# Gate and up of a hybrid decoder block: a phase's third pair of weight tiles is issued behind the reads of the last phase's banks

## The chip, the core and the metric

The kernel runs on one core of one Trainium2 chip. The metric is the device time of one execution in microseconds (us); the time before is the median of three runs. The engines are TensorE (PE, with its weight loads as PEld), VectorE (DVE), ScalarE (ACT), GpSimd (POOL) and SyncE (SP). Each works through its own queue of instructions in the order in which they were written out, and the queues meet through semaphores.

## The reference

The reference is one layer of a decoder block in float32, with 512 tokens and a model width of 2048: a mixer of two head groups, a cross attention over 256 memory tokens, and a SwiGLU. What the change touches is the first half of the SwiGLU:

```
hf = rms_norm(x, g_ffn)
gg, uu = jnp.split(hf @ w_gu, 2, axis=-1)        # w_gu: 2048 x 11264
return x + (jax.nn.silu(gg) * uu) @ w_down        # w_down: 5632 x 2048
```

## The kernel before

The products of a large matrix are taken with seven block products in place of eight (a scheme of Strassen's kind), so weights are first added and subtracted among each other, and the results are put together from several banks. Each product is made in three matmuls to keep float32 accuracy: every operand is split into a high and a low part in the matmul's type (`split`, L128 on ACT for the cast to the high part, L129 on DVE for the low part), and `mm3` (L171 to L173) adds high x high, high x low and low x high. In a row of the profile a tile `qh` is thus a high part and `ql` a low part; `qh` has five buffers and `ql` four.

Gate and up is the loop `for n in range(NB)` (L1204), eleven turns of 512 columns of gate and 512 of up. A turn has two phases, each a call of `phase` (L1135). A phase goes over eight pairs of rows of the weights, `kp` = 0 to 7. The document calls what belongs to one `kp` a pair: pair 0, 1, 2 and so on, so that the third pair is pair 2 (`kp == 2`).

In the first phase `weights_1` (L1108) loads 768 KB for a pair into a tile `raw` (three buffers), subtracts in place (L1111), makes a split of 1024 columns (a), adds (L1113), keeps a copy of the sum (L1115), and makes a second split of 1024 columns (b). A pair then has four products of six matmuls, 24 in all, into the banks "s", "mm", "t" and "mm"/"o". In the second phase `weights_2` (L1119) loads 512 KB, subtracts the kept sum (L1122), and makes one split of 1024 columns and one of 512; a pair has three products, 18 matmuls, which are added onto three of the same sets of banks.

In a phase the pairs 0 and 1 are multiplied together, product by product; then each later pair follows by itself. At the end of the first phase ACT copies a bank (L1214) and DVE adds up the others (L1215, L1217, L1219, two instructions each). At the end of the second phase ACT applies the SiLU to one set of banks (L1229) and DVE adds the others onto sums kept in SBUF (L1231, L1233, two instructions each); L1235 to L1239 finish the values of gate times up. The second phase of a turn also turns the results of the turn before (`turn`, L1166 to L1181), stores them, and starts sums of quarters of `w_down` on POOL's queue (L1195, L1200).

The order of the instructions on each engine is not written by hand. A planner makes it when the program is built: it takes an instruction whose inputs and buffers it expects to be ready, by priority. Priority is the place in the program, moved forward by an offset: a pair's loads and splits are 150 places ahead (`AHEAD`), the reads of the banks at the end of a phase 170 (`EVICT`). Each engine then works in that order, whatever is in fact ready.

Of the kernel before, what the change touches and what calls it, by code (L numbers as in the profile page):

```python
# [13 lines left out]
AF = mybir.ActivationFunctionType  # L14
# [12 lines left out]
AHEAD = 150  # L27
# [28 lines left out]
def hybrid_block(ctx: ExitStack, tc: tile.TileContext, x_t, mem_t, sv, cmat, umask, w_a, w_r67, w_v, w_vg, w_v3,  # L56
                 w_vsw, w_gk2, w_c1, w_c2, w_out, w_cq, w_ck, w_cv, w_co, w_gu, w_down, y_t):
    nc = tc.nc
    V, S, G, PE = nc.vector, nc.scalar, nc.gpsimd, nc.tensor
# [14 lines left out]
    def small(tag, bufs):  # L74
        return sb([128, 32], tag, bufs)
# [7 lines left out]
    def bank(tag):  # L83
        return psp.tile([128, 512], F32, name=tag, tag=tag, bufs={"mm": 3, "s": 2, "t": 2, "o": 1}[tag])
# [54 lines left out]
    class Weights:  # L139
# [9 lines left out]
        def load(self):  # L149
            a = len(self.parts) * self.cut  # L150
            n = min(self.cut, self.cols - a)
            if self.raws:
                raw = sb([128, 1280], *self.raws[len(self.parts)])
            else:
                raw = sb([128, 1024], "w", 2)
            hi, lo = sb([128, 1024], "wh", 3, F32R), sb([128, 1024], "wl", 3, F32R)
            for b in range(0, n, self.step):
                c = slice(b, min(b + self.step, n))
                nc.sync.dma_start(raw[:, c], self.src[:, a + c.start:a + c.stop])
                split(hi[:, c], lo[:, c], raw[:, c])  # L160
            self.parts.append((hi, lo))
# [13 lines left out]
    def part(pair, a, n):  # L175
        return pair[0][:, a:a + n], pair[1][:, a:a + n]
# [50 lines left out]
    def token_norm_col(ss, n, tiles):  # L227
        ps = bank("s")
        for i in range(tiles):
            mm(ps[:, i:i + 1], ss[:, 128 * i:128 * i + 128], one, start=True, stop=True)  # L230
        rc = const.tile([128, 8], F32, name="rc", tag="rc", bufs=4)[:, :tiles]
        inv_rms(rc, ps[:, :tiles], n, const.tile([128, 32], F32, name="rt", tag="rt", bufs=1)[:, :tiles])
        return rc
# [192 lines left out]
    rc2 = small("rc2", 1)[:, :NT]  # L426
# [581 lines left out]
    def sb1(tag, dt=F32):  # L1008
        return pool1.tile([128, COLS2.get(tag, 512)], dt, name=tag, tag=tag, bufs=BUFS2[tag])
# [5 lines left out]
    def split_cols(raw, a, n):  # L1015
        hi, lo = sb1("qh", F32R), sb1("ql", F32R)
        split(hi[:, :n], lo[:, :n], raw[:, a:a + n])
        return hi, lo
# [31 lines left out]
    def sb2(tag, dt=F32):  # L1050
        return pool2.tile([128, COLS2.get(tag, 512)], dt, name=tag, tag=tag, bufs=BUFS2[tag])
# [56 lines left out]
    def weights_1(n, kp):  # L1108
        raw = sb1("raw")
        nc.sync.dma_start(raw[:, :1536], w_gu[n, kp, :, 512:2048])  # L1110
        V.tensor_sub(raw[:, 0:1024], raw[:, 0:1024], raw[:, 512:1536])  # L1111
        a = split_cols(raw, 0, 1024)
        V.tensor_add(raw[:, 1536:2048], raw[:, 0:512], raw[:, 1024:1536])  # L1113
        kept[kp] = sb1("T2")
        S.copy(kept[kp], raw[:, 1536:2048])  # L1115
        b = split_cols(raw, 1024, 1024)
        return part(b, 512, 512), part(b, 0, 512), part(a, 0, 512), part(a, 512, 512)

    def weights_2(n, kp):  # L1119
        raw = sb1("raw")  # L1120
        nc.sync.dma_start(raw[:, :1024], w_gu[n, kp, :, 0:1024])
        V.tensor_sub(raw[:, 1024:1536], raw[:, 0:512], kept[kp])  # L1122
        a = split_cols(raw, 0, 1024)
        b = split_cols(raw, 1024, 512)
        return part(a, 0, 512), part(b, 0, 512), part(a, 512, 512)

    def product(banks, kp, a, w, start, stop, again):
        for i in range(2):
            mm3(banks[i], part(combos[kp], 256 * a + 128 * i, 128), w, start=start, stop=stop, again=again)
# [2 lines left out]
    PHASE_1 = (4, 0, 5, 3)  # L1132
    PHASE_2 = (1, 2, 6)

    def phase(load, banks, plan, middle, last, fresh, ahead, extra):  # L1135

        ws = {}

        def weights(kp):
            with tc.high_priority(offset=AHEAD if kp > 1 else ahead):  # L1140
                ws[kp] = load(kp)

        for kp in range(2):
            weights(kp)
        for p, a in enumerate(plan):
            for kp in range(2):
                product(banks[p], kp, a, ws[kp][p], fresh and kp == 0, False, not fresh)
        for kp in range(2, KP):
            weights(kp)
            for p in last if kp == KP - 1 else middle:  # L1150
                product(banks[p], kp, plan[p], ws[kp][p], False, kp == KP - 1, not fresh)
            for go in extra.get(kp, ()):
                go()
# [6 lines left out]
    def turn(hs, n, k, tag="s"):  # L1160
        def go():
            ps = [bank(tag), bank(tag)]
            for f in range(2):
                c = 256 * k + 128 * f
                for i in range(NT):
                    PE.transpose(ps[f][:, 128 * i:128 * i + 128], hs[i][:, c:c + 128], ident)  # L1166

            e, o, a, b = [sb1("T2") for _ in range(4)]
            S.copy(e, ps[0])
            S.copy(o, ps[1])  # L1170
            x, y = slice(0, 256), slice(256, 512)
            h = V.tensor_sub(a[:, x], e[:, y], o[:, y])
            V.tensor_sub(b[:, x], e[:, x], e[:, y])
            V.tensor_sub(a[:, y], a[:, x], e[:, x])
            V.tensor_add(b[:, y], o[:, x], a[:, y])
            d = hd[n // 3].rearrange("q (p c) -> q p c", p=7)
            c = 512 * (n % 3) + 256 * k
            S.dma_start(d[:, 0, c:c + 256], e[:, x])
            for p, t in ((1, o), (3, a), (5, b)):
                S.dma_start(d[:, p:p + 2, c:c + 256], t.rearrange("q (p c) -> q p c", p=2))  # L1180
            if n < NB - 1:  # L1181
                add_quarters(2 * n + k, h)
        return go
# [17 lines left out]

    rc2 = []
    hs = None
    for n in range(NB):  # L1204
        b1 = [bank("mm"), bank("mm")]
        bu = [bank("s"), bank("s")]
        b2 = [bank("t"), bank("t")]
        b3 = [bank("mm"), bank("o")]
        phase(lambda kp: weights_1(n, kp), (bu, b1, b2, b3), PHASE_1, (2, 3, 1, 0), (1, 0, 2, 3), True,
              AHEAD if n else 40, {})  # L1210
        u, c22 = [sb2("C") for _ in range(2)], [sb2("C") for _ in range(2)]
        with tc.high_priority(offset=EVICT):
            for i in range(2):
                S.copy(u[i], b1[i])  # L1214
                V.tensor_add(u[i], u[i], bu[i])  # L1215
            for i in range(2):
                V.tensor_add(c22[i], u[i], b2[i])  # L1217
            for i in range(2):
                V.tensor_add(c22[i], c22[i], b3[i])  # L1219
        if n == 0:  # L1220
            rc2 = token_norm_col(ss, D, NT)
        extra = {}
        if hs:
            extra = {2: [turn(hs, n - 1, 0)], 4: [turn(hs, n - 1, 1)]}
        phase(lambda kp: weights_2(n, kp), (b1, b2, b3), PHASE_2, (1, 0, 2), (0, 1, 2), False, AHEAD, extra)
        g1, g2 = [sb2("C") for _ in range(2)], [sb2("C") for _ in range(2)]
        with tc.high_priority(offset=EVICT):
            for i in range(2):
                S.activation(g1[i], b1[i], AF.Silu, scale=rc2[:, i:i + 1])  # L1229
            for i in range(2):  # L1230
                V.tensor_add(g2[i], u[i], b2[i])  # L1231
            for i in range(2):
                V.tensor_add(u[i], u[i], b3[i])  # L1233
        for i in range(2):
            S.activation(g2[i], g2[i], AF.Silu, scale=rc2[:, 2 + i:3 + i])  # L1235
        for i in range(2):
            V.scalar_tensor_tensor(g1[i], u[i], rc2[:, i:i + 1], g1[i], op0=OP.mult, op1=OP.mult)
        for i in range(2):
            V.scalar_tensor_tensor(g2[i], c22[i], rc2[:, 2 + i:3 + i], g2[i], op0=OP.mult, op1=OP.mult)  # L1239
        hs = g1 + g2  # L1240
# [91 lines left out]
    banks = [None, [bank(t) for t in SETS[1]]]  # L1332
# [3 lines left out]
    for step, plan in enumerate(STEPS):  # L1336
# [3 lines left out]
        elif step == 1:  # L1340
            banks = [[bank(t) for t in SETS[r]] for r in rs_]
        elif step == 2:
            banks[1] = [bank(t) for t in SETS[1]]
        else:
            banks = [[bank(t) for t in SETS[r]] for r in rs_]
# [30 lines left out]
        elif step == 2:  # L1376
            u = [sb2("C") for x in range(4)]
# [123 lines left out]
```

## Time and profile before

| | us |
|---|---|
| median of 3 runs (lowest, highest) | 2417.41 (2416.54, 2420.03) |
| the profiled execution | 2416.0 |
| its span, first to last instruction | 2413.9 |
| PE busy | 2325.7 (96%) |
| DVE busy | 1672.6 (69%) |
| ACT busy | 1183.2 (49%) |
| mean granted clock of TensorE | 0.987 of full speed |

Busy time is counted from an instruction's start to its end, with waits left out. Matmuls overlap, so that a busy TensorE is not one at its peak: in the dense stretches of this stage a matmul starts every 0.227 us, though each row gives 0.39 us. A number in brackets behind a row of a timeline is the time for which the engine stood idle before it, and what it waited for. The eleven turns of gate and up lie between about 1048 and 1965 us of the span.

### The profile page before, as it was taken

To read this page: it belongs to the slowest core of one execution; us is meant where nothing else is said; L and a number is where in the kernel's file an instruction comes from. 1 tells how busy PE (TensorE), PEld (TensorE's weight loads), DVE (VectorE), ACT (ScalarE), POOL (GpSimd) and SP (SyncE) were. 2 spreads that over 40 slices of the span, in tenths; PEclk is the share of its full clock that TensorE was granted. 3 is DMA by queue.
4 is the path that set the end of the run, shared out by engine and by line. 5 is a ranking of instruction groups with operands and counts; after the bars stand their busy time and mean duration, and the time that the engine had idled before them with its cause. 6 is when DMAs were issued, how large, how long until landed. Compare 5 with 4: busy or idle time off the path is not lost.

```text
span 2413.9 us, 29614 instructions
## 1 busy us (share of the span) xinstructions
PE 2325.7 (96%) x10954; PEld 1923.0 (80%) x10954; DVE 1672.6 (69%) x2522; ACT 1183.2 (49%) x1787; POOL 130.3 (5%) x187
## 2 busy tenths in 40 slices
PE   8999999999999999979999999999999998999999
PEld 7798888888887887768877787777778777888887
DVE  6647876667786335698777777778877875775685
ACT  6633454556675225565444444444544456444542
POOL 0000000000000000110001000100100000000000
PEclk9999999999999999989999999999999999999999
DMA  6432233423225332564557666765766689676763
GB/s 232 150 107 70 84 114 122 146 81 101 92 92 175 122 130 85 165 197 144 175 174 222 201 187 202 224 185 175 234 201 191 201 306 331 229 255 227 256 252 144
DMA packets 131681, 421.33 MB, mean 175 GB/s; under 512 B 13488, under 2 KB 33968, under 8 KB 127312
## 3 DMA queue, kind: packets, MB, share of 16 engines
q1 hardware_dynamic: 82048, 325.05, 38.8%
q0 software_dynamic: 26064, 70.00, 12.2%
q10 hardware_dynamic: 23424, 24.39, 2.9%
q8 instruction: 86, 1.41, 0.2%
q14 instruction: 59, 0.48, 0.1%
HBM read 376.92 MB, written 84.67 MB: 191 GB/s over the span
## 4 chain that ended last, share of the span: by engine, by line
PE 79%; DMA 9%; DVE 6%; issue 3%; ACT 2%; SPq 0%; ACTq 0%; DVEq 0%; POOLq 0%
PE mm L173 14%; PE mm L172 14%; PE mm L171 14%; DMA raw<-w_gu 5%; PE t L172 4%; PE t L173 4%; PE t L171 4%; PE s L172 4%; PE s L173 3%; PE s L171 3%; PE o L172 3%; PE o L171 3%; DVE ql L129 3%; PE o L173 3%; DMA raw<-w_down 1%
## 5 line engine op out<-in xcount | busy, mean ns | idle before, releaser
L128 ACT CAST qh<-raw 128x1024 fp32r<-128x1024 f32 (+1 forms) x520 | 503.8, 979 | 484.2 <-PE o L173 145.0
L129 DVE TENSOR_TENSOR ql<-raw,qh 128x1024 fp32r<-128x1024 f32 (+1 forms) x520 | 581.2, 1131 | 124.9 <-PE mm L172 46.9
L171 PE MATMUL mm<-X,wh 128*128 128x512 f32 x784 | 312.7, 399 | 2.9 <-ACT X L128 2.9
L173 PE MATMUL mm<-X,wl 128*128 128x512 f32 x784 | 308.7, 394 | 0.1
L172 PE MATMUL mm<-X,wh 128*128 128x512 f32 x784 | 308.3, 393 | 0.0
L172 PE MATMUL mm<-ql,P 128*128 128x512 f32 x770 | 303.4, 394 | 2.9 <-DVE ql L129 2.9
L173 PE MATMUL mm<-qh,P 128*128 128x512 f32 x770 | 302.5, 393 | 0.0
L129 DVE TENSOR_TENSOR wl<-w,wh 128x1024 fp32r<-128x1024 f32 (+2 forms) x154 | 184.5, 1201 | 166.6 <-ACT wh L128 166.1
L171 PE MATMUL mm<-qh,P 128*128 128x512 f32 x770 | 299.7, 392 | 0.0
L128 ACT CAST wh<-w 128x1024 fp32r<-128x1024 f32 (+2 forms) x154 | 158.2, 1029 | 246.1 <-PE mm L172 138.5
L171 PE MATMUL t<-qh,P 128*128 128x512 f32 x484 | 190.9, 395 | 14.7 <-ACT qh L128 14.7
L172 PE MATMUL t<-ql,P 128*128 128x512 f32 x484 | 190.0, 393 | 4.6 <-DVE ql L129 4.3
L173 PE MATMUL t<-qh,P 128*128 128x512 f32 x484 | 189.2, 391 | 0.0
L172 PEld LDWEIGHTS mm<-ql,P 128*128 128x128 f32 x770 | 146.3, 190 | 35.4 <-DVE ql L129 4.8
L173 PEld LDWEIGHTS mm<-X,wl 128*128 128x128 f32 x784 | 148.0, 189 | 32.5 <-DVE wl L129 1.4
L171 PEld LDWEIGHTS mm<-X,wh 128*128 128x128 f32 x784 | 148.1, 189 | 30.7 <-ACT X L128 3.3
L173 PEld LDWEIGHTS mm<-qh,P 128*128 128x128 f32 x770 | 146.3, 190 | 30.6
L172 PEld LDWEIGHTS mm<-X,wh 128*128 128x128 f32 x784 | 148.3, 189 | 27.8 <-DVE X L129 0.4
L171 PEld LDWEIGHTS mm<-qh,P 128*128 128x128 f32 x770 | 145.2, 189 | 30.8 <-DVE T L1321 0.2
L1111 DVE TENSOR_TENSOR raw<-raw 128x1024 f32<-128x1024 f32 x88 | 107.6, 1223 | 84.7 <-DMA raw<-w_gu 84.4
L172 PE MATMUL s<-ql,P 128*128 128x512 f32 x352 | 142.4, 405 | 24.4 <-DVE ql L129 24.3
L171 PE MATMUL s<-qh,P 128*128 128x512 f32 x352 | 138.4, 400 | 8.4 <-ACT qh L128 8.4
(455 smaller groups left out, 4077.9 us busy)
## 6 DMA issues: line engine op xcount, KB each, us to landing
raw<-w_gu SPq DMA_DIRECT2D x88, 768.0 KB, 5.5
raw<-w_gu SPq DMA_DIRECT2D x88, 512.0 KB, 3.4
raw<-w_down SPq DMA_DIRECT2D x88, 512.0 KB, 4.7
td<-w_down POOLq DMA_DIRECT2D x66, 512.0 KB, 9.5
w<-w_a SPq DMA_DIRECT2D x60, 512.0 KB, 3.5
raw<-td SPq DMA_DIRECT2D x22, 1024.0 KB, 4.8
h<-T ACTq DMA_DIRECT2D x66, 256.0 KB, 5.4
w<-w_out SPq DMA_DIRECT2D x32, 512.0 KB, 3.4
```

Of the source, the lines that this page charges most:

```text
L128: S.copy(hi, src)
L129: V.tensor_sub(lo, src, hi)
L171: mm(ps, lhs[0], rhs[0], start=start, stop=False, skip_group_check=again)
L172: mm(ps, lhs[0], rhs[1], start=False, stop=False, skip_group_check=again)
L173: mm(ps, lhs[1], rhs[0], start=False, stop=stop, skip_group_check=again)
L1111: V.tensor_sub(raw[:, 0:1024], raw[:, 0:1024], raw[:, 512:1536])
```

## The change

`phase` takes a `fence`, the last instructions on ACT and on DVE that read the banks of the phase before. When it comes to pair 2 it makes every instruction of that pair that runs on the engine of a fence instruction take its place behind it in that engine's queue (`tc.issue_after`). There is no new wait: it is an order alone. The first phase of the first turn has no fence.

```diff
-    def phase(load, banks, plan, middle, last, fresh, ahead, extra):
+    def phase(load, banks, plan, middle, last, fresh, ahead, extra, fence=()):
 
         ws = {}
 
         def weights(kp):
-            with tc.high_priority(offset=AHEAD if kp > 1 else ahead):
+            with tc.high_priority(offset=AHEAD if kp > 1 else ahead), ExitStack() as behind:
+                if kp == 2:
+                    for i in fence:
+                        behind.enter_context(tc.issue_after(i.ins))
                 ws[kp] = load(kp)
...
+    fence = ()
     for n in range(NB):
...
         phase(lambda kp: weights_1(n, kp), (bu, b1, b2, b3), PHASE_1, (2, 3, 1, 0), (1, 0, 2, 3), True,
-              AHEAD if n else 40, {})
+              AHEAD if n else 40, {}, fence)
...
-                S.copy(u[i], b1[i])
+                fa = S.copy(u[i], b1[i])
...
-                V.tensor_add(c22[i], c22[i], b3[i])
+                fv = V.tensor_add(c22[i], c22[i], b3[i])
...
-        phase(lambda kp: weights_2(n, kp), (b1, b2, b3), PHASE_2, (1, 0, 2), (0, 1, 2), False, AHEAD, extra)
+        phase(lambda kp: weights_2(n, kp), (b1, b2, b3), PHASE_2, (1, 0, 2), (0, 1, 2), False, AHEAD, extra,
+              (fa, fv))
...
-                S.activation(g1[i], b1[i], AF.Silu, scale=rc2[:, i:i + 1])
+                fa = S.activation(g1[i], b1[i], AF.Silu, scale=rc2[:, i:i + 1])
...
-                V.tensor_add(u[i], u[i], b3[i])
+                fv = V.tensor_add(u[i], u[i], b3[i])
+        fence = fa, fv
```

## Rows read from the trace of the kernel before

**Rows 1.** Table of stretches, turns n = 1 and 2: busy us by engine, PEclk, DMA, GB/s.

```profile
1128.00:1206.00 78.00, 78.00 (x353) 64.42 (x352) 61.04 (x76) 37.31 (x48) 2.30 (x4) 1.00 0.50 163
1206.00:1289.30 83.30, 79.12 (x353) 64.45 (x352) 63.60 (x79) 39.46 (x51) 7.81 (x10) 1.00 0.67 199
```

**Rows 2.** List of waits, 1050 to 1970: who waited for whom, us, times, longest.

```profile
PE s L172 <- DVE ql L129: 24.3, 14, 3.6
PE s L171 <- ACT qh L128: 8.4, 8, 1.1
```

**Rows 3.** Timeline of DVE, turn 1 to 2: start, us, instruction [idle before].

```profile
1205.29 1.22 DVE L129 TENSOR_TENSOR ql<-raw,qh 128x1024 fp32r<-128x1024 f32 x1
1208.47 1.23 DVE L1111 TENSOR_TENSOR raw<-raw 128x1024 f32<-128x1024 f32 x1 [1.97 <-DMA raw<-w_gu]
1209.61 1.28 DVE L1231 TENSOR_TENSOR C<-C,t 128x512 f32<-128x512 f32 x2
...
1212.01 3.49 DVE L129 TENSOR_TENSOR ql<-raw,qh 128x1024 fp32r<-128x1024 f32 x3
1215.41 0.69 DVE L1113 TENSOR_TENSOR raw<-raw 128x512 f32<-128x512 f32 x1
```

**Rows 4.** Timeline of TensorE, the same change, and the last of the nine.

```profile
1205.99 0.39 PE L171 MATMUL s<-qh,P 128*128 128x512 f32 x1
1206.56 0.50 PE L172 MATMUL s<-ql,P 128*128 128x512 f32 x1 [0.18 <-DVE ql L129]
...
1209.06 0.73 PE L171 MATMUL s<-qh,P 128*128 128x512 f32 x2 [1.08 <-ACT qh L128]
...
1211.46 0.39 PE L171 MATMUL t<-qh,P 128*128 128x512 f32 x1
1214.41 0.50 PE L172 MATMUL s<-ql,P 128*128 128x512 f32 x1 [2.57 <-DVE ql L129]
...
1221.57 0.39 PE L171 MATMUL t<-qh,P 128*128 128x512 f32 x1
...
1890.49 0.50 PE L172 MATMUL s<-ql,P 128*128 128x512 f32 x1 [2.83 <-DVE ql L129]
```

**Rows 5.** Timeline of DVE and TensorE, turn 0 to 1.

```profile
1124.92 1.22 DVE L1111 TENSOR_TENSOR raw<-raw 128x1024 f32<-128x1024 f32 x1
...
1127.92 1.28 DVE L1231 TENSOR_TENSOR C<-C,t 128x512 f32<-128x512 f32 x2
...
1131.67 0.41 PE L172 MATMUL s<-ql,P 128*128 128x512 f32 x1
```

**Rows 6.** Timeline of ACT, turn 1 to 2.

```profile
1207.97 1.04 ACT L128 CAST qh<-raw 128x1024 fp32r<-128x1024 f32 x1
...
1210.96 1.03 ACT L128 CAST qh<-raw 128x1024 fp32r<-128x1024 f32 x1
```

**Rows 7.** Table of stretches, behind the wait of turn 2: TensorE, PEclk, DMA, GB/s.

```profile
1298.70:1302.00 3.30, 3.25 (x8) 0.53 0.67 247
```

**Rows 8.** Timeline of DVE, first to second phase of turn n = 5.

```profile
1505.35 0.69 DVE L1122 TENSOR_TENSOR raw<-raw,T 128x512 f32<-128x512 f32 x1 [2.35 <-DMA raw<-w_gu]
...
1511.28 0.69 DVE L129 TENSOR_TENSOR ql<-raw,qh 128x512 fp32r<-128x512 f32 x1
1511.88 0.69 DVE L1122 TENSOR_TENSOR raw<-raw,T 128x512 f32<-128x512 f32 x1
```

**Rows 9.** Timeline of TensorE, the same change.

```profile
1512.02 0.50 PE L172 MATMUL t<-ql,P 128*128 128x512 f32 x1 [0.29 <-DVE ql L129]
...
1516.00 0.39 PE L171 MATMUL t<-qh,P 128*128 128x512 f32 x1
```

**Rows 10.** DMA at 1206 to 1209: stretch, SP's issue, its landing; page, all such loads.

```profile
1206.00:1209.00 3.00, 1.80 (x7) 1.00 0.98 310
1206.53 0.33 SPq L1110 DMA_DIRECT2D raw<-w_gu  x1
raw<-w_gu SPq DMA_DIRECT2D x1, 768.0 KB, 7.7
...
raw<-w_gu SPq DMA_DIRECT2D x88, 768.0 KB, 5.5
```

## Prediction

> **What bounds the kernel now.** I read the page first: TensorE is busy for 96% of the span, so a DVE or ACT edit can only pay where TensorE stands still or runs slowly. The table of stretches comes next, cut so that each stretch is one turn of the gate-and-up loop. The second turn (n = 1) takes 78.0 us with TensorE busy for all of it; the next takes 83.3 us for the same 352 or so matmuls [rows 1]. The eleven turns fill 1048 to 1965 us, and all but the first two look like the second row there. The list of waits says what the difference is: inside this stage TensorE waits 24.3 us in 14 waits for a low-part split on DVE (L129) before a matmul into the "s" banks, and 8.4 us for a high-part cast on ACT [rows 2]. The five short ones of those 14 are like the 0.18 us at 1206.56 and together hold 0.87 us; the other nine are 1.50 to 3.57 us, one at each change from the second phase of a turn to the first phase of the next, n = 1 to 9; the first and the last of them are shown [rows 4]. They add up to 23.45 us.
>
> What holds DVE there is seen in its timeline at the first of them [rows 3]. DVE finishes the split of pair 0 at about 1206.4 and then stands for 1.97 us at L1111, the first subtraction of the new phase's pair 2, whose transfer has not landed. Only behind it come the four additions that read the old banks (L1231, L1233), and behind those the splits of pair 1, which TensorE needs. TensorE meanwhile works through what it has and stops at 1211.7 until the second of these splits is done [rows 4]. So the wait that ends last is a transfer that TensorE does not need for another 10 us, ahead of two splits that it needs at once, on one in-order queue.
>
> The change from n = 0 to n = 1 is the control: there the same subtraction finds its data (no wait before 1124.92), the additions start at 1127.92, and the matmul that waits elsewhere starts at 1131.67 with no wait before it [rows 5].
>
> **The change part by part.**
> *Second phase to first phase, DVE.* For pair 2, one L1111 (1.22 us), one L1113 and two L129 must now follow the last L1233. Of these only L1111 stands ahead of it today (L1113 at 1215.41 and pair 2's splits are behind already [rows 3]); so one instruction moves at each of these nine changes, and its wait moves with it. At n = 0 to 1 its L1113 moves too, and nothing there waits for either: 0. Without it DVE is free at 1205.29 + 1.14 = 1206.43 (1.14 us is the spacing of such instructions: 1208.47 to 1209.61). TensorE's last matmuls into the old banks end about then (the first "s" matmul starts at 1205.99 [rows 4]). From the first L1231 to the matmul that waited is 1214.41 - 1209.61 = 4.80 us: four additions at 0.6, two splits at 1.14 and the semaphore. So this matmul's data would be ready at 1206.43 + 4.80 = 1211.23. TensorE comes to it at 1211.46 + 0.23 = 1211.69: 0.46 us later, so the wait of 2.57 us goes whole. I worked out the other eight in the same way; the 4.80 us is the same each time, and ready stands 0.46 to 0.50 us before need each time. The casts that these splits read are done in time: pair 1's second one runs 1207.97 to 1209.0 [rows 6], and its split would start at 1210.0.
> Gain: 23.45 us, and 0.15 us at each of the nine for the restart (1211.46 to 1214.41 is 2.95 us, where 2.57 + 0.23 = 2.80 would do), 1.4 us.
>
> *The clock.* After four of the nine (n = 2, 3, 5, 6) the granted clock is at the 1.2 GHz level for a while: in 1298.7 to 1302.0 it is 0.53 and 8 matmuls take 3.30 us [rows 7], where 8 x 0.227 = 1.81 would do, a loss of 1.5 us. With no wait there is nothing for the clock to fall after. Gain 4 x 1.5 = 6.0 us; between 0, if it falls after what waits remain, and 6.0. I take 6.0, since in TensorE's timeline no wait of 1.1 us or less in this stage is followed by such a stretch.
>
> *What is late next.* Pair 2's own work. Behind the two splits L1111 would start at 1211.2 (its transfer landed by 1208.47) and end at 1212.3; cast to 1213.4; split done by 1214.7. TensorE reaches pair 2 today at 1221.57 [rows 4], 7.16 us after the matmul that waited, so it would at 1211.69 + 7.16 = 1218.85: over 4 us of cover, and about 4 us in the turn with the longest wait. If that cover were gone, each microsecond late would cost nine. The third wait of this part, 1.08 us for a cast on ACT at 1209.06 [rows 4], stays: nothing before that cast moves.
>
> *First phase to second phase, DVE.* Here L1122 of pair 2 moves from ahead of L1215 (1505.35) to behind L1219 and pair 1's last split, to about 1511.9, where pair 3's L1122 stands now [rows 8]. Its wait (about 2 us at nine of the eleven changes) leaves the front of the queue, but the split of pair 1 between the two L1215 waits for a buffer that TensorE frees only at about 1507.2, so what follows keeps its time. TensorE has next to no wait to give back: 0.29 us at 1512.02 [rows 9]. Pair 2's small split needs L1122: 1511.9 + 0.7, cast 0.6, split 0.7, with one split in between, about 1514.3; TensorE asks for it at 1516.00 [rows 9]. Cover 1.7 us. Bounds: a gain of 0.1 to 0.5 us at three changes, 1 us; a loss of up to 1 us at each of eleven, if pair 3's subtraction and its wait came in between. I take 0.
>
> *ACT and the queues of transfers.* On ACT the first cast of pair 2 already follows both L1229 (cast at 1210.96, L1229 done by 1208.0 [rows 6]) and, in the other phase, both L1214: 0. SP's loads of pair 2 are in the block too, but the fence instructions are on DVE and ACT, so I take SP's order as it is. If the loads did go behind, they would land some 6 us later, about 1214.3, and pair 2 would be split by 1217.6, still before 1218.85: 0 at that change, at most 1 us at others.
>
> **Sum.** 23.45 + 1.4 + 6.0 = 30.9 us off the profiled execution (2416.0 us; its span 2413.9). The median of the three runs is 2417.41, 1.4 us above it. Forecast 2417.4 - 30.9 = 2386.5; I say 2387.
>
> **Rivals.**
> 1. *Half way.* The list puts pair 2's L1111 right behind the additions but ahead of pair 1's splits. Then the splits wait for 1206.43 + 2.40 + 1.14 and the matmul's data come at 1212.37: 0.68 us of wait remains at seven changes, 1.3 at the two with the latest transfers, 7.3 us in all. Gain 30.9 - 7.3 = 23.6, 2393.8. For it: L1111 would be ready. Against it: pair 1's splits come earlier in the program, and today three splits run in a row while pair 2's L1113 is ready and waits its turn [rows 3]. 0.13.
> 2. *Given back to the transfers.* At these changes the 16 DMA engines are busy to 0.98 and a 768 KB load takes 7.7 us, against a median of 5.5 over all 88 [rows 10]. If loads do not move forward with TensorE, it waits for a later pair instead. Pair 3's load, issued at 1206.53 [rows 10], lands at 1214.2 whatever TensorE does; with subtraction, cast and split it is ready by 1217.7, and needed at 1218.85 + 5.44 (24 matmuls) = 1224.3. It would have to land 6.6 us later to be felt at all. If it decided everywhere the 30.9 us would come back as later waits: 2417, and 2412 if a sixth of them stayed saved. 0.05.
> The Trainium skill says that transfers started by different engines run on the same 16 DMA engines and interleave (DMA: Bandwidth & Descriptors, Issuing engines are not separate DMA queues); by it the loads of POOL and ACT around the change hold SP's, the trace's 0.98 agrees, and by it alone the time would be this rival's.
> 3. *Slower.* With pair 2 fenced, pair 3, which is not, is the next to be put ahead: its L1111 lands in front of pair 1's splits. Its load lands at 1214.2, so the splits would end at 1214.2 + 1.14 + 2.40 = 1217.7, 3.3 us later than today; over nine changes 30 us, 2447. It decides from a place ahead of pair 1's second split on. Against it: pair 3's load can only start when the split of pair 0 has freed its tile (1206.53), so it is ready after the additions are. 0.08.
> 4. *No effect*: the freed place on DVE is filled with other work of the same length, 2417. 0.05.
> 5. *More*: the list of TensorE is laid anew with the earlier splits, and the 8.4 us of waits for ACT [rows 2] go too: 2377. 0.05.
>
> **How the numbers follow.** Forecast 0.64, with its own range 2381 to 2392; the rivals as given. The range for 8 in 10 holds the forecast and the first rival: 2379 to 2402. What a measurement of this kernel can tell from no change is about 0.2%, 4.8 us. Faster: 0.64 + 0.13 + 0.05 + part of the second rival, 0.86; same 0.06; slower 0.08.
>
> **What would show it.** In the changed kernel's trace: at each change to a first phase, L1231 follows the split of pair 0 with no wait for a transfer, and the third L1111 of a phase stands behind L1233 and two splits; TensorE's waits for L129 ahead of "s" matmuls fall from 24.3 us to about 1; the granted clock of the turns n = 2 to 9 rises to 0.99 or more, but for the one stretch near 1629; turns take about 80 us for 83; the ACT wait of 1.08 us stays. I am wrong if a matmul of pair 1 still waits over 0.5 us for a split, or if waits of pair 2 or 3 appear behind the change.

## The result and the profile after

| us | before | after |
|---|---|---|
| median (lowest to highest) | 2417.41 (2415.84 to 2431.18), 5 runs | 2400.88 (2390.94 to 2408.62), 5 runs |
| ratio to before, 95% interval | 1 | 0.9932 (0.9907 to 0.9956) |
| the profiled execution, its span | 2416.0, 2413.9 | 2406.62, 2404.5 |
| mean granted clock | 0.987 | 0.989 |

The change makes the kernel 16.5 us faster, by the medians. The forecast was 30.4 us faster; 2400.88 lies inside the range, near its upper end. The profiled execution of the changed kernel is one of its slower ones, with a span 9.4 us shorter than before; so the rows below show where some 9 us came from, not 16.5.

The waits of TensorE and of the subtractions on DVE in the changed kernel, 1050 to 1950 us (who waited for whom: us, times, longest):

```profile
DVE raw L1111 <- DMA raw<-w_gu: 93.8, 36, 4.7
DVE raw L1122 <- DMA raw<-w_gu: 53.3, 53, 3.4
PE mm L172 <- DVE ql L129: 12.7, 8, 2.9
PE t L172 <- DVE ql L129: 9.8, 10, 1.7
PE s L171 <- ACT qh L128: 8.5, 9, 1.1
PE s L172 <- DVE ql L129: 0.9, 5, 0.2
```

The same lines in the kernel before:

```profile
DVE raw L1111 <- DMA raw<-w_gu: 84.4, 41, 5.0
DVE raw L1122 <- DMA raw<-w_gu: 84.0, 63, 3.4
PE t L172 <- DVE ql L129: 4.3, 4, 2.8
PE mm L172 <- DVE ql L129: 1.4, 2, 0.8
```

The 24.3 us of [rows 2] are 0.9 us now: the nine waits are gone, all of them, and the wait for ACT is as it was. But two lines have grown: before "mm" matmuls TensorE waited 1.4 us for splits in the kernel before and waits 12.7 us now, before "t" matmuls 4.3 and 9.8 us. So 16.8 us came back against 23.4 that went: the sum of TensorE's waits here fell from 38.4 to 31.9 us.

DVE at the same change of turns as in [rows 3] (start, us, instruction, idle before it):

```profile
1204.22 1.22 DVE L129 TENSOR_TENSOR ql<-raw,qh 128x1024 fp32r<-128x1024 f32 x1
1205.36 0.68 DVE L1236 TENSOR_TENSOR C<-C,t 128x512 f32<-128x512 f32 x1
1205.96 1.22 DVE L129 TENSOR_TENSOR ql<-raw,qh 128x1024 fp32r<-128x1024 f32 x1
...
1208.89 1.22 DVE L129 TENSOR_TENSOR ql<-raw,qh 128x1024 fp32r<-128x1024 f32 x1
1210.02 1.22 DVE L1111 TENSOR_TENSOR raw<-raw 128x1024 f32<-128x1024 f32 x1
1213.99 1.23 DVE L1111 TENSOR_TENSOR raw<-raw 128x1024 f32<-128x1024 f32 x1 [2.75 <-DMA raw<-w_gu]
1215.13 0.68 DVE L1113 TENSOR_TENSOR raw<-raw 128x512 f32<-128x512 f32 x1
1215.73 1.22 DVE L129 TENSOR_TENSOR ql<-raw,qh 128x1024 fp32r<-128x1024 f32 x1
...
1217.47 1.22 DVE L129 TENSOR_TENSOR ql<-raw,qh 128x1024 fp32r<-128x1024 f32 x1
...
1227.84 1.23 DVE L1111 TENSOR_TENSOR raw<-raw 128x1024 f32<-128x1024 f32 x1 [4.48 <-DMA raw<-w_gu]
1228.98 1.22 DVE L129 TENSOR_TENSOR ql<-raw,qh 128x1024 fp32r<-128x1024 f32 x1
```

The additions (L1231 and L1233 before, L1236 and L1238 now) follow pair 0's split at once, and pair 1's splits run at 1205.96 and 1208.89, ahead of pair 2's L1111 at 1210.02. This is what was wanted. Right behind it, though, stands the L1111 of pair 3, which has no fence, and it waits 2.75 us for its transfer ahead of pair 2's L1113 and both its splits. The later one, 1227.84, is pair 5's; it waits 4.48 us ahead of pair 4's splits.

TensorE and SP in the changed kernel (SP's issue of pair 5's load, and its landing after 9.1 us):

```profile
1209.73 0.39 PE L173 MATMUL mm<-qh,P 128*128 128x512 f32 x1
1210.16 0.50 PE L172 MATMUL s<-ql,P 128*128 128x512 f32 x1
...
1218.02 0.39 PE L171 MATMUL t<-qh,P 128*128 128x512 f32 x1
...
1230.26 0.50 PE L172 MATMUL t<-ql,P 128*128 128x512 f32 x1 [0.97 <-DVE ql L129]
...
1248.22 0.50 PE L172 MATMUL mm<-ql,P 128*128 128x512 f32 x1 [1.35 <-DVE ql L129]
...
1218.72 0.33 SPq L1110 DMA_DIRECT2D raw<-w_gu  x1
...
raw<-w_gu SPq DMA_DIRECT2D x1, 768.0 KB, 9.1
```

The same load in the kernel before:

```profile
1219.06 0.33 SPq L1110 DMA_DIRECT2D raw<-w_gu  x1
...
raw<-w_gu SPq DMA_DIRECT2D x1, 768.0 KB, 6.0
```

TensorE is at pair 2 at 1218.02, 3.55 us ahead of 1221.57 in [rows 4] (1.08 us of it was gained before this change of turns: its first "s" matmul starts at 1204.91 for 1205.99). Pair 5's load starts only 0.34 us ahead, because it needs the weight tile of pair 2, which is free when pair 2's last split is done (1217.47 + 1.14 = 1218.6); and it takes 9.1 us for 6.0. So TensorE meets the wait at 1230.26 that it did not meet before. The other new kind is at 1248.22, at the end of the first phase, where pair 7's split stands behind the L1122 of pair 1 of the next phase.

Adding up, over the 88 rows of each line, the idle time that a transfer ended, by the pair that the row belongs to:

| us | pair 0 | 1 | 2 | 3 | 4 | 5 | 6 | 7 |
|---|---|---|---|---|---|---|---|---|
| L1111 before | 29.2 | 8.6 | 18.2 | 0.5 | 0.7 | 23.8 | 0.2 | 3.2 |
| L1111 after | 28.6 | 8.7 | 0 | 23.6 | 0.6 | 22.4 | 7.0 | 3.0 |
| L1122 before | 5.8 | 25.5 | 21.2 | 0 | 6.3 | 7.2 | 8.2 | 9.7 |
| L1122 after | 3.9 | 26.2 | 0 | 0 | 2.3 | 9.0 | 6.0 | 5.8 |

A row's pair is told by its place among the eight of its phase. In first phases the wait has moved from pair 2 to pair 3, whole. In second phases pair 2's has gone.

### The profile page after: what moved, and what is told of

Its sections match the earlier page's. It is cut to its first block, busy times and chain, and to the rows that moved or that the text cites. A ratio compares the mean times of both kernels' runs of the same rounds, so it can differ in the third digit from the quotient of the medians.

```text
span 2404.5 us, 29605 instructions
## 1 busy us (share of the span) xinstructions
PE 2322.6 (97%) x10954; PEld 1917.3 (80%) x10954; DVE 1671.1 (69%) x2522; ACT 1179.2 (49%) x1787; POOL 130.5 (5%) x187
## 5 line engine op out<-in xcount | busy, mean ns | idle before, releaser
L172 PE MATMUL mm<-ql,P 128*128 128x512 f32 x770 | 302.6, 393 | 12.7 <-DVE ql L129 12.7
L172 PEld LDWEIGHTS mm<-ql,P 128*128 128x128 f32 x770 | 145.4, 189 | 46.7 <-DVE ql L129 16.5
L1111 DVE TENSOR_TENSOR raw<-raw 128x1024 f32<-128x1024 f32 x88 | 107.4, 1222 | 94.0 <-DMA raw<-w_gu 93.8
L1115 ACT COPY T<-raw 128x512 f32<-128x512 f32 x88 | 54.7, 621 | 200.1 <-DVE raw L1113 200.1
```

Source lines behind the costliest of these rows:

```text
L172: mm(ps, lhs[0], rhs[1], start=False, stop=False, skip_group_check=again)
```

## Experiments

Diffs are against the changed kernel. Each was timed against the kernel before in the same session; the ratios are to be compared, as the kernel before ran 2417 to 2424 us in the four sessions.

### The two halves of the change alone

```diff
# e1: fence in the first phases only
-    phase(..., PHASE_2, ..., extra, (fa, fv))
+    phase(..., PHASE_2, ..., extra)
# e2: fence in the second phases only
-    phase(..., PHASE_1, ..., {}, fence)
+    phase(..., PHASE_1, ..., {})
```

> Only the first phases of the turns have a fence; in the second phases pair 2 is free as before. Theory A (the whole gain comes from the subtraction of pair 2 at the nine changes from second to first phase, and what is given back comes from the order alone): the move in the second phase is worth nothing, so 2401 +- 5 us, as with the whole change; the waits of s matmuls for DVE stay at about 1 us. Theory B (the fence of the second phases is what makes the new waits of 12.7 us ahead of mm matmuls at the end of first phases): these go back to about 1.4 us, and 2385 to 2391.

Measured: 2418.96 us, ratio 0.9996 (0.9975 to 1.0018). Both theories missed.

> Only the second phases have a fence; at the change from second to first phase everything is as before. Theory A: 2417 +- 5 us, and the waits of s matmuls for DVE stay at 24 us. Theory B: slower than before by some 11 us, 2428, with the mm waits of 12 us there.

Measured: 2418.22 us, ratio 0.9984 (0.9968 to 1.0000): within theory A's range, with TensorE's "s" waits at 26.5 us. So the half that removes the nine waits is worth nothing alone, the half that I had put at nothing is worth nothing or little alone, and the two together are worth 0.7%. The waits of the first-phase half, 1050 to 1950 us (its profiled execution is one of the slower of its twelve, 2429.07 us):

```profile
DVE raw L1122 <- DMA raw<-w_gu: 102.6, 66, 4.4
...
PE mm L172 <- DVE ql L129: 23.0, 12, 2.6
PE t L172 <- DVE ql L129: 16.1, 13, 3.6
...
PE s L172 <- DVE ql L129: 1.1, 6, 0.2
```

The "s" waits are gone here too; 23.0 and 16.1 us stand in their place. Its DVE at the end of a first phase shows how (n = 4):

```profile
1419.36 0.69 DVE L1122 TENSOR_TENSOR raw<-raw,T 128x512 f32<-128x512 f32 x1 [4.36 <-DMA raw<-w_gu]
1419.97 2.35 DVE L129 TENSOR_TENSOR ql<-raw,qh 128x1024 fp32r<-128x1024 f32 x2
1424.91 0.69 DVE L1122 TENSOR_TENSOR raw<-raw,T 128x512 f32<-128x512 f32 x1 [2.59 <-DMA raw<-w_gu]
1425.52 2.35 DVE L129 TENSOR_TENSOR ql<-raw,qh 128x1024 fp32r<-128x1024 f32 x2
1429.95 0.69 DVE L1122 TENSOR_TENSOR raw<-raw,T 128x512 f32<-128x512 f32 x1 [2.08 <-DMA raw<-w_gu]
1430.56 0.69 DVE L129 TENSOR_TENSOR ql<-raw,qh 128x512 fp32r<-128x512 f32 x1
```

The subtractions of pairs 0, 1 and 2 wait one after the other, and each has splits behind it: those of the pairs before, which TensorE needs and whose end frees the tile for the next load. A load of a second phase takes 3.5 us here from its issue (median, 1206 to 1870 us), and it is issued once its tile is free, so a wait that holds the freeing sets up the next wait.

### The other transfers: no sums of quarters

```diff
-            if n < NB - 1:
-                add_quarters(2 * n + k, h)
...                                           # steps 2 and 3 of the last stage load w_down[0], [1] for td
```

> The kernel before without the sums of quarters of w_down on POOL's queue (the last stage reads plain quarters in their place, so its values differ). It measures what the transfers beside the loads cost. Theory A: pair 2's load lands earlier, so that the wait ahead of the additions shrinks by itself: the nine s waits fall below 1 us each; 2385 to 2395. Theory C (the DMA engines' supply limits this stage, and order does not matter): the same.

Measured: 2358.28 us, ratio 0.9736 (0.9709 to 0.9763), faster than expected. TensorE still waits 13.1 us in nine waits before "s" matmuls, the longest 2.6 us, where each was expected to fall below 1 us:

```profile
PE s L172 <- DVE ql L129: 13.1, 9, 2.6
```

> The changed kernel without the same sums. Theory A and theory C both expect the waits of the first phases behind pair 3 to go. They part in the difference to the kernel before without sums: theory A, in which the transfers' lateness is needed for either order to hurt, expects the change to be worth little there, 0 to 8 us; theory C, in which the change frees 31 us and the transfers take half of it back, expects 25 to 31 us.

Measured: 2341.56 us, ratio 0.9677 (0.9651 to 0.9702). The change is worth 0.6% of the time of before here too, some 14 us by the ratios, between what the theories expected. In this trace no wait of TensorE for DVE is left in gate and up; what remains is this:

```profile
PE s L171 <- ACT qh L128: 0.5, 1, 0.5
```

So without the sums TensorE gets no new wait for splits in gate and up: nothing is given back there. A load of 768 KB takes 4.2 us (median, 1206 to 1870 us) in both kernels without sums, 6.0 before and 6.9 after with them.

The Trainium skill says that the transfers which different engines start run on the same 16 DMA engines and interleave (DMA: Bandwidth & Descriptors, Issuing engines are not separate DMA queues). The trace agrees: POOL's sums make SP's loads 1.8 to 2.7 us longer.

### The order on DVE, one step further

These kernels keep a handle to the last split (`low[0]`, set in `split`; `tail` is its value when a phase begins), so their lines count two to four higher.

```diff
# e3                                           # e6: kp > 2 for kp == 3
+                if kp == 3 and fresh:
+                    behind.enter_context(tc.issue_after(low[0].ins))
# e4
+                if kp == 1 and fence:
+                    behind.enter_context(tc.issue_after(tail.ins))
# e7: e4 and e6 together
```

> The changed kernel, and in first phases pair 3's DVE work stands behind pair 2's last split. Theory A (order: the wait for a transfer has moved from pair 2's subtraction, 18.2 us, to pair 3's, 23.6 us, which stands ahead of pair 2's splits and so holds the buffer that pair 5's load needs): pair 3's wait shrinks and the waits of t matmuls in the middle of first phases, 7 us, go: 2393 us; but pair 4's subtraction stands next in line and may take the wait over, 2400. Theory C (supply: the load of pair 5 is late whatever the order): no change, 2401.

Measured: 2382.90 us, ratio 0.9846 (0.9829 to 0.9862): more than theory A had hoped for. L1111 (L1113 here) waits 2.4 us at pair 3 for 23.6; some of the wait has moved on, to 11.8 us at pair 4 (0.6 before this edit) and 15.1 at pair 6 (7.0).

> The changed kernel, and pair 1's DVE work of each phase stands behind the last split of the last phase's pair 7. Theory A: the wait of L1122 of pair 1 (26 us in all) no longer stands ahead of the splits of pair 7 that TensorE needs, so the waits of 12.7 us ahead of mm matmuls at the ends of first phases go, and those of t matmuls at the ends of second phases: 2386 to 2390. Theory C: pair 1's data is late itself, the waits turn up at pair 1 in the next phase: 2398 to 2401.

Measured: 2381.23 us, ratio 0.9832 (0.9818 to 0.9846): theory A and a little more. The edit does not touch the middle of the first phases, and yet TensorE's waits there went as well:

```profile
PE s L173 <- ACT qh L130: 8.5, 9, 1.1
...
PE s L174 <- DVE ql L131: 4.6, 4, 1.6
PE mm L174 <- DVE ql L131: 2.6, 1, 2.6
...
PE t L174 <- DVE ql L131: 0.6, 1, 0.6
```

The 12.7 us before "mm" matmuls are 2.6, as the edit is to do, and the 9.8 before "t" matmuls are 0.6; pair 3's L1111 waits 9.4 us in all for 23.6. Lateness is handed on from one place of a turn to the next. A little turns up at the start of the next phase, as theory C has it: 4.6 us before "s" matmuls, for 0.9.

> The changed kernel, and in first phases the DVE work of every pair from 3 on stands behind the last split of the pair before it. Theory A: no subtraction in a first phase waits for a transfer ahead of a split that is ready; the t waits of 7 us go, the mm waits at the ends of first phases stay: 2393. Against it: each pair's cast can now only start behind the split of the pair before, which may hold TensorE: up to 24 us slower. Theory C: 2401.

Measured: 2378.27 us, ratio 0.9822 (0.9798 to 0.9847). That is 15 us less than theory A's 2393. The fear that the chain would hold TensorE did not come true: L1111 waits for transfers only at pairs 0, 1 and 3 (30.8, 4.2, 1.3 us), and TensorE's waits for splits before "mm", "t" and "s" are 3.3, 1.4 and 0.8 us.

> Both of the last two edits together. Theory A: their gains add, 2378 to 2384. Theory C: 2398 to 2401.

Measured: 2376.07 us, ratio 0.9814 (0.9796 to 0.9832): the lowest median of all with the sums in place (its interval overlaps those of e4 and e6), 45 us less than before in its session, and faster than the changed kernel by 1.2% by the ratios. The two edits do not add up, as each removes most of what the other removes.

> The version with the chain of the first phases and pair 1 behind pair 7's last split, without the sums of quarters of w_down on POOL's queue (the last stage reads plain quarters in their place, so its values differ). The same edits on the changed kernel with the sums gained 25 us (2401 to 2376). Theory D: without the sums no load is late behind a fence, as the changed kernel without sums has no wait of TensorE left for splits, so the edits are worth nothing there: 2342 +- 4. If the order had a worth of its own, TensorE's waits for ACT would still fall: 2330 to 2337.

Measured: 2342.43 us, ratio 0.9665 (0.9648 to 0.9682), the same as the changed kernel without sums (0.9677), as theory D expects: a better order is worth 1.2% where loads are late, and nothing where they are not.

### What the second phases' fence does

```diff
# f1: in second phases, pair 2 behind pair 0's last split alone
-                    for i in fence:
+                    for i in fence if fresh else firsts[:1]:
...                                           # firsts: the last split of each pair of the phase
```

> First phases as in the changed kernel. In second phases pair 2's L1122 stands behind pair 0's last split alone, and still ahead of the additions that read the banks. The fence of the first phases alone gave 2419, both fences 2401, so the second phases' fence is worth 18 us and not the 0 of the prediction. Theory D (buffers: a subtraction that waits for its load ahead of pair 0's last split keeps pair 0's weight tile from being freed, so the load of pair 3 starts later by that wait, and the lateness goes on from load to load): the whole worth stays, 2401 +- 5, and the waits of subtractions for loads in second phases fall to about 55 us from 103. Theory E (the bank reads: what matters is that the additions run earlier): the worth is gone, 2419 +- 5, and those waits stay at about 100 us.

Measured: 2413.26 us, ratio 0.9960 (0.9946 to 0.9974), half way between 0.9996 and 0.9932; neither theory's number. Its waits, 1050 to 1950 us (the profiled execution is the fastest of its seven, 2403.34 us):

```profile
DVE raw L1124 <- DMA raw<-w_gu: 93.1, 65, 4.1
...
PE mm L174 <- DVE ql L131: 16.0, 10, 3.2
...
PE t L174 <- DVE ql L131: 12.0, 6, 4.3
```

L1122 (L1124 here) of pair 2 still waits 13.9 us, now ahead of the additions and of pair 1's splits. So, by the ratios, about half of this fence's worth is bought by letting pair 0's split, which frees a tile, go first; the interval reaches into that of the changed kernel, so the share is rough. Whether the other half comes from pair 1's splits, which free the next tile, or from the bank reads themselves, this run cannot tell, and it stays open.

## Why the prediction was half right

**Right.** The nine waits, their cause and their removal: 23.45 us forecast, all gone. The data of the matmul that waited were ready when the sum said: it starts at 1210.16, right behind the end of its split (1208.89 + 1.22 = 1210.11), and that is 1211.24 in the times of the trace before, which are 1.08 us later here; the forecast was 1211.23. The margin of 0.46 us was not there. TensorE's list was laid anew, and it comes to this matmul three matmuls earlier, at 1209.73 + 0.23 = 1209.96, so that the matmul starts 0.2 us late at each of the nine changes. The wait for ACT stayed (8.4 and 8.5 us). The four stretches at the lower clock level went too, and so did the one near 1629 that I had expected to stay; one came new, behind the wait of 2.92 us at 1418.59 (granted clock 0.72, third number from the right):

```profile
1418.00:1424.00 6.00, 5.42 (x17) 0.72 0.49 174
```

**Wrong: "what is late next".** I put pair 2's splits done by 1214.7, with over 4 us of cover. They were done at 1218.6 (1219.7 in the times before), since pair 3's L1111 took the place behind pair 2's and waited 2.75 us there. This is the mechanism of the third rival one pair later: I had asked only whether pair 3 could come ahead of pair 1's splits, and said rightly that it could not. Pair 2's cover held, and TensorE did not wait for pair 2; but I had followed one pair only. Its late end holds the tile for pair 5's load. In the second rival I took it that a load 6.6 us later would be needed to be felt, and had worked this out for pair 3, the one load that was already on its way. The loads behind it start when a tile is freed, and that moved by 0.34 us where TensorE moved by 3.55.

**Wrong: first phase to second phase, taken as 0.** I read the cover there from TensorE's times before, in which it comes to the end of the first phases 1.5 to 3.6 us late because of the very wait that the change removes. With the wait gone, the subtractions of pairs 1 and 2 stand ahead of splits that TensorE needs: its waits before "mm" matmuls, at the ends of first phases, are 23.0 us with the first fence alone and 12.7 with both, for 1.4 before. The term should have been a loss, in part bought back by the second fence. That the 11.3 us lost here are the size of the bound of 1 us at each of eleven is luck, as that bound was set for pair 3's subtraction, and it is pair 1's that stands in the way. By the times, the first-phase half of the change alone gives everything back (0.9996), and both together keep 0.68%, about half of what was forecast.

The second rival, given back to the transfers, had 0.05. About half of the gain went that way, but not since the 16 engines had no more to give: the chain of the first phases moves the same bytes and takes 1.1% less time than the changed kernel, by the ratios. Two things were needed: an order on DVE that makes loads start late, and the sums beside the loads, as without them the same order gives nothing back.

**In the range by luck.** The forecast's own range, up to 2392, was missed. The part of the range that holds 2400.88 was there for the first rival, which did not happen: pair 2's L1111 stands behind pair 1's splits. Of the other signs, turns n = 2 to 9 were to take about 80 us; from one first "s" matmul to the next they take 83.5 on average, for 84.5 before.

## What to carry to other kernels

An instruction that waits for a load holds all that stands behind it on its in-order engine; where that includes the last reader of an earlier load's tile, it also holds the next load, and the lateness goes round. Moving one such instruction leaves the next one in its place: look for the whole series (here, every subtraction ahead of the split of the pair before) before pricing the first. And when a wait is removed, do the cover of every later step anew with the times that TensorE will then have, not with those of the trace.

## What the runs showed that was not expected

Leaving out the sums of quarters of `w_down`, which run beside gate and up on POOL's queue, makes the kernel before 62 us faster (2420.61 to 2358.28), more than any order on DVE. Not all of that lies in gate and up. In the profiled executions that stage, from its first "s" matmul to the first one behind it, takes 914.7 us before (1050.02 to 1964.75) and 876.9 without the sums (1045.09 to 1922.02), 37.8 us less; another 14.8 us lie behind the stage, where the kernel without sums also loads other matrices, so that part is not the price of the sums alone. The chain with pair 1 behind pair 7, with all its sums, takes 876.3 us for the stage (1046.86 to 1923.13, in the fastest of its four executions): there the order gives back about as much as leaving out the sums does.

The runs of one kernel also spread unevenly: 2405 to 2433 us in 12 runs of the first-phase half, 2412 to 2421 in 12 of the second-phase half, 2413 to 2430 in 23 of the kernel before. Why is not shown.
